# Sample mixer's tail: scores stored, the dense blocks' top-k moved into it, and their transposed input handed on through memory

## The chip, the cores and the metric

One core of one Trainium2 chip runs the whole program. The metric is the device time of one execution in microseconds (us).

## The reference, cut to what matters

Two layers, each a token mixer and then an expert channel mixer (PEER). 128 prompt tokens and 512 sample tokens go through both; the change concerns the sample tokens alone. For the channel mixer each token has 8 heads; a head has two queries of 128 numbers, each is scored against 128 keys, the best 16 of each half are combined and the best 16 pairs name 16 experts. So a token reads 128 rows of `u` and 128 rows of `v`.

```python
def peer(h, wq, sub_keys, u, v):
    ...
    def one_block(xt):                      # 128 tokens
        q = (xt @ wq).reshape(PEER_BLOCK, PEER_HEADS, 2, PEER_HALF)
        s = jnp.einsum('thpd,pnd->thpn', q, sub_keys).astype(jnp.float32)
        s1, i1 = lax.top_k(s[:, :, 0], PEER_TOPK)
        s2, i2 = lax.top_k(s[:, :, 1], PEER_TOPK)
        cand = (s1[..., :, None] + s2[..., None, :]).reshape(PEER_BLOCK, PEER_HEADS, PEER_TOPK * PEER_TOPK)
        sc, ci = lax.top_k(cand, PEER_TOPK)
        idx = jnp.take_along_axis(i1, ci // PEER_TOPK, axis=-1) * N_KEYS + jnp.take_along_axis(i2, ci % PEER_TOPK, axis=-1)
        g = jax.nn.softmax(sc, axis=-1)
        a = jax.nn.gelu(jnp.einsum('td,thkd->thk', xt, u[idx]).astype(jnp.float32))
        return jnp.einsum('thk,thkd->td', (g * a).astype(xt.dtype), v[idx])
...
    x = layer_norm(ALPHA * x + gate1 * mix, ln1_g, ln1_b)
    h = x * (1.0 + scale2) + shift2
    x = layer_norm(ALPHA * x + gate2 * peer(h, peer_wq, peer_sub_keys, peer_u, peer_v), ln2_g, ln2_b)
```

## The kernel before, in words

**Blocks.** The 512 sample tokens are four blocks of 128. Blocks 0 and 1 (`ROWS`, called r0 and r1 here) are done row by row: GpSimd (POOL) gathers one `u` or `v` row per token into a tile `gat` (128x1024, half a megabyte), and VectorE (DVE) takes one dot product (L917) or one multiply-add (L947) with it. A block has 128 `u` rows and 128 `v` rows, and six `gat` tiles (`GB`). Blocks 2 and 3 (`DENSE`, called d0 and d1) are done densely: TensorE (PE) multiplies their 256 tokens with all 128 x 128 experts, 128 experts ("a key") at a time. `uc` is such a slab of `u`, `hp` its product; a `v` slab is accumulated into `vacc`. In between DVE and PE build the sparse weights: DVE makes `A`, `eq` and `bw` for 16 tokens, PE multiplies them to `Gp` (L1070), DVE multiplies that into the activations `Q` (L1075). `spread(c)` does this for a quarter of the keys in 16 such groups, 64 groups a layer. The first group needs the top-k of d0 and d1 finished: their indices go through `ki`, `kf` and a PE transpose `kT`.

**A front** is the top-k of one block: for each of 8 heads two times `top16` (L797 to L802: MAX8, FIND_INDEX8, MATCH_REPLACE8, MAX8, FIND_INDEX8) over the scores `sc`, then the 50 candidate pairs, a third `top16`, and three operations on 800 numbers (`oh`, `oh`, `xf`) that fetch the index. Heads are done in groups: r0 in groups of 1, 1, 2, 2, 2 (`LEAD`), the others in two groups of 4. A group ends with its indices `idx`, which the gathers need.

**The tail** of the sample mixer computes the queries: for each head, `qp` from eight slabs of weights that ScalarE (ACT) and DVE or POOL split into a high part `wh` and a low part `wl`, copied by ACT to `q` and stored to `qTd` in DRAM. While it runs, DVE does the front of r0, whose scores PE takes straight from `q` ("near"), and the first `U0` = 56 rows of `u` for r0.

**The dense stage** follows: `dense` loads the `h2` rows of d0 and d1, transposes them on PE into `h2Td`, and starts with the `hp` of 32 keys. The fronts of d0, d1 and r1 lie in this stage. Each head of such a front loads `qT` from DRAM, PE multiplies it with the keys into `sc` in PSUM (L825), and DVE's `top16` reads that. The `sc` tiles share two PSUM buffers with `hp`, `Gp` and `kT`, and PE takes its instructions in order.

**Order.** The program is written as generators that `weave` interleaves by shares of a nominal length; a scheduler at build time then moves instructions within what their data allow. The result is one fixed order for each engine and queue. In layer 0 the prompt's mixer of layer 1 is woven into the dense stage; in layer 1 the dense stage stands alone and ends the program.

In the profile, layer 0 has its tail at 1428 us and its first `bw` at 1852 us, the seventeenth `bw` (the first of the second quarter) at 1961 us, and its last `vacc` at 2986 us. In layer 1 these are 4064, 4488, 4612 and 5405 us.

## Time and profile before

| | us |
|---|---|
| three timed runs | 5451.07, 5448.35, 5431.43 |
| their median | 5448.35 |
| the profiled execution, its own time | 5425.23 |
| its span, first to last instruction | 5423.5 |
| mean granted TensorE clock of the span | 0.887 of full speed |

The profile is of one execution, 23 us faster than the median of the three timed ones. The busy time of an engine is the time in which at least one of its instructions was running; what an engine waited for is inferred from semaphores. A wait counts only where that engine is the one that everything else waits for.

### The profile page before, as it was taken

To read this page: it belongs to the slowest core of one execution; us is meant where nothing else is said; L and a number is where in the kernel's file an instruction comes from. 1 tells how busy PE (TensorE), PEld (TensorE's weight loads), DVE (VectorE), ACT (ScalarE), POOL (GpSimd) and SP (SyncE) were. 2 spreads that over 40 slices of the span, in tenths; PEclk is the share of its full clock that TensorE was granted. 3 is DMA by queue.
4 is the path that set the end of the run, shared out by engine and by line. 5 is a ranking of instruction groups with operands and counts; after the bars stand their busy time and mean duration, and the time that the engine had idled before them with its cause. 6 is when DMAs were issued, how large, how long until landed. Compare 5 with 4: busy or idle time off the path is not lost.

```text
span 5423.5 us, 71661 instructions
## 1 busy us (share of the span) xinstructions
PE 4479.1 (83%) x26668; PEld 3365.0 (62%) x26668; DVE 3891.9 (72%) x8020; ACT 1038.4 (19%) x1876; POOL 2199.4 (41%) x1632
## 2 busy tenths in 40 slices
PE   7979878877766789799999477688977458998998
PEld 5658766755655657567674355588765347675643
DVE  4242578887699987948565999963258999979682
ACT  4231223412212101110000312255221010000000
POOL 0000026675255541544431576610115657255440
PEclk8989977888878889899999778789988779998999
DMA  5325669898489887899995788820447989699985
GB/s 185 118 70 179 235 225 327 305 338 297 171 318 348 317 317 258 310 357 334 382 344 206 244 309 297 290 91 29 131 146 271 329 305 362 225 399 325 409 327 197
DMA packets 472734, 1440.70 MB, mean 266 GB/s; under 512 B 55232, under 2 KB 123968, under 8 KB 472384
## 3 DMA queue, kind: packets, MB, share of 16 engines
q0 software_dynamic: 221184, 805.40, 40.5%
q1 hardware_dynamic: 251200, 630.71, 33.0%
q8 instruction: 209, 3.42, 0.2%
q14 instruction: 141, 1.16, 0.1%
HBM read 1391.29 MB, written 44.63 MB: 265 GB/s over the span
## 4 chain that ended last, share of the span: by engine, by line
PE 39%; DVE 26%; DMA 15%; issue 14%; POOL 4%; ACT 2%; SPq 0%; DVEq 0%; POOLq 0%; ACTq 0%
PE vacc L1096 7%; DVE gat L917 7%; PE gt L156 6%; PE proj L156 6%; DMA gat<-in_pv,idx 5%; PE hp L156 4%; DMA gat<-in_pu,idx 4%; POOL gat L900 4%; DVE acc L947 4%; PE po L156 3%; PE qp L156 2%; DMA v<-in_pv 2%; PE s L156 1%; PE gqk L156 1%; DVE A L1055 1%
## 5 line engine op out<-in xcount | busy, mean ns | idle before, releaser
L900 POOL DMA_INDIRECT gat<-in_pu,idx x768 | 982.3, 1279 | 884.9 <-DVE gat L917 378.7
L900 POOL DMA_INDIRECT gat<-in_pv,idx x768 | 989.4, 1288 | 765.1 <-DVE acc L947 472.9
L947 DVE SCALAR_TENSOR_TENSOR acc<-gat,dots,acc 128x1024 f32<-128x1024 f32 x762 | 1006.3, 1321 | 168.3 <-DMA gat<-in_pv,idx 156.1
L917 DVE SCALAR_TENSOR_TENSOR gat<-gat,h 128x1024 f32<-128x1024 f32 x768 | 948.4, 1247 | 110.8 <-DMA gat<-in_pu,idx 109.5
L156 PE MATMUL hp<-h2Td,uc 128*128 128x256 f32 x4096 | 942.5, 391 | 79.8 <-DVE wk L800 49.6
L1096 PE MATMUL vacc<-v,Q 128*128 128x512 f32 x2048 | 923.3, 604 | 17.2 <-DMA v<-in_pv 17.2
L156 PEld LDWEIGHTS hp<-h2Td,uc 128*128 128x128 f32 x4096 | 795.3, 196 | 200.2 <-DVE wk L800 52.3
L141 POOL TENSOR_TENSOR wl<-w,wh 128x1024 fp32r<-128x1024 f32 x92 | 227.5, 2473 | 1450.0 <-ACT wh L139 1279.5
L1096 PEld LDWEIGHTS vacc<-v,Q 128*128 128x128 f32 x2048 | 384.1, 193 | 459.4 <-issue 435.4
L139 ACT ACTIVATE wh<-w 128x1024 fp32r<-128x1024 f32 x184 | 194.4, 1058 | 631.9 <-PE proj L156 299.1
L1009 ACT ACTIVATE Q<-hp 128x512 f32<-128x512 f32 x128 | 76.4, 597 | 1069.6 <-PE hp L156 1069.3
L156 PE MATMUL proj<-wh,hTh 128*128 128x256 f32 x896 | 265.6, 296 | 5.6 <-DVE sgo L497 2.9
L156 PE MATMUL proj<-wl,hTh 128*128 128x256 f32 x896 | 264.7, 295 | 5.5 <-POOL wl L141 5.4
L156 PE MATMUL proj<-wh,hTl 128*128 128x256 f32 x896 | 262.8, 293 | 0.0
L1070 PEld LDWEIGHTS <-A 128*128 128x128 bf16 x6144 | 172.8, 97 | 125.7 <-DVE bw L1063 63.2
L156 PE MATMUL po<-V,pT 128*128 128x64 f32 x1600 | 237.9, 294 | 9.9 <-ACT pT L639 9.8
L156 PEld LDWEIGHTS po<-V,pT 128*128 128x128 f32 x1600 | 229.2, 217 | 24.9 <-ACT pT L639 16.7
L1070 PE MATMUL Gp<-bw,A 128*128 128x32 bf16 x6144 | 175.8, 177 | 73.3 <-DVE bw L1063 64.1
L141 DVE TENSOR_TENSOR wl<-w,wh 128x1024 fp32r<-128x1024 f32 x92 | 121.0, 1315 | 158.7 <-ACT wh L139 148.4
L629 DVE TENSOR_REDUCE nm<-s 128x1 f32<-128x768 f32 (+1 forms) x160 | 131.0, 820 | 139.9 <-PE s L156 138.5
L156 PEld LDWEIGHTS proj<-wh,hTh 128*128 128x128 f32 x896 | 176.9, 197 | 20.4 <-issue 16.2
L156 PEld LDWEIGHTS proj<-wl,hTh 128*128 128x128 f32 x896 | 176.9, 197 | 20.4 <-issue 13.8
(297 smaller groups left out, 7355.5 us busy)
## 6 DMA issues: line engine op xcount, KB each, us to landing
uc<-in_put SPq DMA_DIRECT2D x256, 512.0 KB, 7.0
v<-in_pv SPq DMA_DIRECT2D x256, 512.0 KB, 6.7
w<-in_win SPq DMA_DIRECT2D x208, 512.0 KB, 5.1
w<-in_adaw SPq DMA_DIRECT2D x96, 512.0 KB, 5.7
w<-in_wq SPq DMA_DIRECT2D x64, 512.0 KB, 5.8
w<-in_wgo SPq DMA_DIRECT2D x32, 512.0 KB, 5.5
w<-in_wao SPq DMA_DIRECT2D x32, 512.0 KB, 5.2
w<-in_wout SPq DMA_DIRECT2D x32, 512.0 KB, 5.5
```

What stands on the lines that cost most here:

```text
L139: nc.scalar.activation(wh, r, AF.Copy)
L141: (nc.vector, nc.gpsimd)[i].tensor_sub(wl, r, f32(wh))
L156: nc.tensor.matmul(out, lt, rt, start=(i == 0), stop=(i == n - 1))
L629: nc.vector.tensor_reduce(nm, s[:, 0:KEYS], axis=AX.X, op=OP.max, negate=True)
L900: i = nc.gpsimd.indirect_dma_start(out=t, out_offset=None, in_=src, in_offset=bass.IndirectOffsetOnAxis(ap=self.res[b][0][:, k:k + 1], axi ...
L917: nc.vector.scalar_tensor_tensor(u, u, 1.0, h2, op0=OP.mult, op1=OP.mult, accum_out=dots[:, k:k + 1])
L947: nc.vector.scalar_tensor_tensor(acc, v, w_, acc, op0=OP.mult, op1=OP.add)
L1009: nc.scalar.activation(q[:, i:i + 2, :].rearrange("p i t -> p (i t)"), t, AF.Gelu_apprx_tanh)
L1055: nc.vector.tensor_tensor(a.rearrange("p t (i w) -> p t i w", w=2), pairs[:, None].to_broadcast([128, TG, NK // 2, 2]), i1[:, sl, None, :] ...
L1070: nc.tensor.matmul(t[:, j * CI:(j + 1) * CI], a[:, j, :], bw[:, j, q, :], start=(q == 0), stop=(q == 2))
L1096: nc.tensor.matmul(accs[i][:, s * 512:(s + 1) * 512], w[:, j, i * 128:(i + 1) * 128], v[:, s * 512:(s + 1) * 512], start=(key == 0), stop= ...
```

## The change

It touches the sample tokens alone, in both layers. Lines in this section and in the order rows of the change are those of the changed file.

- In the tail, PE multiplies each head's `q` with the keys at once, for all four blocks (L812). ACT copies the scores from PSUM to a tile `sc` in SBUF, and stores those of r1, d0 and d1 to `scd` in DRAM, a DMA that ACT issues itself (L821). The `qTd` stores of the sample and the `qT` loads go.
- The fronts of d0, d1 and r1 load these scores back into `scs` (two buffers), also from ACT's queue (L852); their `top16` reads SBUF.
- d0 and d1 are done in four groups of two heads (`NEXT`). Three of the four groups of each are written into the tail, between the groups of r0; the fourth opens the dense stage.
- Of r0's `u` rows 24 in place of 56 are written into the tail (`U0`).
- The tail copies the transposed `h2` of d0 and d1 a second time from PSUM (`hc`, ACT), stores it, and `dense` loads it with one DMA of 1 MB. The `h2` rows of d0 and d1 are no longer stored, loaded or transposed again.

```diff
...
 LEAD = (1, 1, 2, 2, 2)
+NEXT = (2, 2, 2, 2)
-FF = (0.05, 0.1, 0.3, 0.46)
+FF = (0.01, 0.02, 0.3, 0.46)
 DENSE = (2, 3)
...
-U0 = 56
+U0 = 24
...
-    x_dram, x1_dram, h2_dram, tops = {}, {}, {}, {}
+    x_dram, x1_dram, h2_dram, h2t_dram, tops = {}, {}, {}, {}, {}
...
         x1d = dram.tile([T, D], F32, name=f"x1d{tr}{l}")
         h2d = dram.tile([T, D], F32, name=f"h2d{tr}{l}")
         x1_dram[tr, l], h2_dram[tr, l] = x1d, h2d
+        if tr:
+            h2t_dram[l] = dram.tile([128, ND, len(DENSE) * 128], F32, name=f"h2t{l}")
...
         if tr == 0 and l == 0:
             yield from ada(l, (GATE1, SCALE2, SHIFT2, GATE2), W)
-        qTd = dram.tile([2 * PH, 128, T], F32, name=f"qTd{tr}{l}")
-        tops[tr, l] = qTd
+        if tr:
+            scd = dram.tile([nb, 128, PH * 2 * NK], F32, name=f"scd{l}")
+            tops[tr, l] = scd
+        else:
+            qTd = dram.tile([2 * PH, 128, T], F32, name=f"qTd{tr}{l}")
+            tops[tr, l] = qTd
         with mkp("out") as op:
             r = op.tile([128, nb, D], F32, name="r")
             x = op.tile([128, nb, D], F32, name="x")
...
                     h2 = spare("h2")
                     nc.vector.tensor_mul(h2, rb, s2)
                     nc.vector.tensor_add(h2, h2, sh)
-                    nc.sync.dma_start(h2d[b * 128:(b + 1) * 128, :], h2)
+                    kept = tr == 1 and b in DENSE
+                    if not kept:
+                        nc.sync.dma_start(h2d[b * 128:(b + 1) * 128, :], h2)
                     for j0 in range(0, ND, jg):
                         t = ptile("h2t")
                         for j in range(jg):
...
                             put_split(dst, t3)
                         else:
                             evac(dst[0], t3)
+                        if kept:
+                            hc = spare("hc")
+                            nc.scalar.activation(hc[:, 0:jg * 128], t, AF.Copy)
+                            i = DENSE.index(b)
+                            nc.sync.dma_start(h2t_dram[l][:, j0:j0 + jg, i * 128:(i + 1) * 128],
+                                              hc[:, 0:jg * 128].rearrange("p (j t) -> p j t", j=jg))
                     yield 6
                 for b in range(nb):
                     rb, xb = r[:, b, :], x[:, b, :]
...
             for h in range(PH):
                 w = W(wq[l, h])
                 t = ptile("qp")
+                qs = []
                 for k in range(2):
                     projT(t[:, k * off:k * off + T], w, k, h2T)
-                    q = hp.tile([128, T], F32, tag="q", bufs=2 + 2 * tr, name="q")
+                    q = hp.tile([128, T], F32, tag="q", bufs=2 + tr, name="q")
                     if tr:
                         nc.scalar.activation(q, t[:, k * off:k * off + T], AF.Copy)
                     else:
                         evac(q, t[:, k * off:k * off + T])
-                    nc.sync.dma_start(qTd[2 * h + k], q)
-                    lp[l]["q", tr, 2 * h + k] = q
+                        nc.sync.dma_start(qTd[2 * h + k], q)
+                    qs.append(q)
+                if tr:
+                    yield 11
+                    for b0 in range(0, nb, 2):
+                        s = psm("sc", 1)
+                        for i in range(2):
+                            for k in range(2):
+                                nc.tensor.matmul(s[:, (2 * i + k) * NK:(2 * i + k + 1) * NK],
+                                                 qs[k][:, (b0 + i) * 128:(b0 + i + 1) * 128],
+                                                 lp[l]["sk"][:, k, :], start=True, stop=True)
+                        sc = hp.tile([128, 2, 2 * NK], F32, tag="sc", bufs=4, name="sc")
+                        nc.scalar.activation(sc.rearrange("p b n -> p (b n)"), s, AF.Copy)
+                        for i in range(2):
+                            if b0 + i == ROWS[0]:
+                                lp[l]["s", h] = sc[:, i, :]
+                            else:
+                                nc.scalar.dma_start(scd[b0 + i, :, h * 2 * NK:(h + 1) * 2 * NK], sc[:, i, :])
                 lp[l]["qp", tr] = h + 1
-                yield 11
+                yield 3 if tr else 11
             hs.close()
             ys_.close()
...
                 hh = h0 + h
                 assert lp[l]["qp", tr] > hh
                 if near:
-                    qs = [lp[l]["q", tr, 2 * hh + k][:, b * 128:(b + 1) * 128] for k in range(2)]
+                    s = lp[l]["s", hh]
+                elif tr:
+                    s = own.tile([128, 2 * NK], F32, tag="scs", bufs=2, name="scs")
+                    nc.scalar.dma_start(s, tops[tr, l][b, :, hh * 2 * NK:(hh + 1) * 2 * NK])
                 else:
                     qT = sm.tile([128, 2, 128], F32, tag="qT", bufs=CB, name="qT")
                     nc.sync.dma_start(qT, tops[tr, l][2 * hh:2 * hh + 2, :, b * 128:(b + 1) * 128]
                                       .rearrange("k p t -> p k t"))
-                    qs = [qT[:, k, :] for k in range(2)]
-                s = psm("sc", tr)
-                for k in range(2):
-                    nc.tensor.matmul(s[:, k * NK:(k + 1) * NK], qs[k], lp[l]["sk"][:, k, :], start=True, stop=True)
+                    s = psm("sc", tr)
+                    for k in range(2):
+                        nc.tensor.matmul(s[:, k * NK:(k + 1) * NK], qT[:, k, :], lp[l]["sk"][:, k, :],
+                                         start=True, stop=True)
                 for k in range(2):
                     top16(tv[:, h, k, :], ti[:, h, k, :], s[:, k * NK:(k + 1) * NK], NK)
                 yield 2
...
             CI, QB, HI, UB = CIS[self.l], QBS[self.l], HIS[self.l], UBS[self.l]
             per = CI // HI
             h2T = dp.tile([128, ND, T], F32, name="h2Td")
-            for i, b in enumerate(blocks):
-                x = dp.tile([128, D], F32, tag="uv", bufs=UB, name="x")
-                nc.sync.dma_start(x, h2_dram[self.tr, self.l][b * 128:(b + 1) * 128, :])
-                t = psb("h2td")
-                for j in range(ND):
-                    nc.tensor.transpose(t[:, j * 128:(j + 1) * 128], x[:, j * 128:(j + 1) * 128], ident)
-                evac(h2T[:, :, i * 128:(i + 1) * 128], t.rearrange("p (j t) -> p j t", j=ND))
-                yield 4
+            nc.sync.dma_start(h2T, h2t_dram[self.l])
+            yield 4
             Q = {}
             def acts(hf):
...
             parts["p_close", l].close()
             p = Peer(1, l, opener(st_, 0)("sgat"), GB)
             r0, r1 = ROWS
-            d0, d1 = DENSE
             f0, u0 = p.front(r0, LEAD, True), p.u_rows(r0)
+            fd = [p.front(d, NEXT) for d in DENSE]
             def lead():
-                for n in LEAD:
-                    yield from take(m, n)
+                for i, n in enumerate(LEAD):
+                    yield from take(m, 2 * n)
                     yield from take(f0, 3 * n + 1)
+                    if i >= 2:
+                        for f in fd:
+                            yield from take(f, 3 * NEXT[i - 2] + 1)
                 for _ in m:
                     pass
-            yield from weave([(lead(), 160.0, 0.0, 1.0)], [(take(u0, U0), 1.5 * U0, UP, 1.0)])
+            yield from weave([(lead(), 260.0, 0.0, 1.0)], [(take(u0, U0), 1.5 * U0, UP, 1.0)])
             for _ in f0:
                 pass
             ms.close()
...
             yield from weave([(p.dense(p.up, DENSE), 1010.0, DF[0], DF[1])],
                              [(u0, 192.0 - 1.5 * U0, r[0], r[1]), (p.v_rows(r0), 197.0, r[1], r[2]),
                               (p.u_rows(r1), 192.0, r[2], r[3]), (p.v_rows(r1), 197.0, r[3], r[4])],
-                             [(p.front(d0), 50.0, 0.0, f[0]), (p.front(d1), 50.0, f[0], f[1]),
-                              (p.front(r1), 50.0, f[2], f[3])])
+                             [(fd[0], 12.5, 0.0, f[0]), (fd[1], 12.5, f[0], f[1]), (p.front(r1), 50.0, f[2], f[3])])
         fs = parts["fin"] = ExitStack()
         fp = opener(fs, 0)("fin")
         ds.close()
```

What this does to PE's order at the start of layer 1's dense stage. Before, from the tail's last scores on (`qT` are the loaded queries of d0, then d1):

```order
L825 MATMUL sc<-sk,q 128x128 x2
L825 MATMUL sc<-sk,qT 128x128 x2
L995 MATMUL h2td<-ident,x 128x128 x16
L825 MATMUL sc<-sk,qT 128x128 x6
L156 MATMUL hp<-h2Td,uc 128x256 x43
L825 MATMUL sc<-sk,qT 128x128 x2
L156 MATMUL hp<-h2Td,uc 128x256 x5
L825 MATMUL sc<-sk,qT 128x128 x4
L156 MATMUL hp<-h2Td,uc 128x256 x16
```

Here the scores of d0 and d1 (`sc<-sk,qT`) and the transposes of their `h2` (`h2td`) stand between and ahead of the `hp`.

After, the same place up to the transposes of the finished indices:

```order
L157 MATMUL qp<-h2Th,wl 128x512
L812 MATMUL sc<-sk,q 128x128 x8
L157 MATMUL hp<-h2Td,uc 128x256 x256
L1067 MATMUL kT<-ident,kf 128x128 x2
L1068 MATMUL kT<-ident,g 128x128
```

Eight `hp` are one key, so 32 keys stand ahead of `kT`, as before; what has moved is the scores, which now stand in the tail, before the `hp`.

DVE in layer 1, the last rows ahead of the first `bw`. Before, a stretch from the last index of d1 on, in which every second row is one of r0's `v` rows:

```order
L866 CAST idx<-xf 128x64
L947 SCALAR_TENSOR_TENSOR acc<-gat,dots,acc 128x1024
L1033 TENSOR_SCALAR ki<-idx 128x128
L947 SCALAR_TENSOR_TENSOR acc<-gat,dots,acc 128x1024
L1037 CAST kf<-ki 128x128
L947 SCALAR_TENSOR_TENSOR acc<-gat,dots,acc 128x1024
```

Here nothing of r1 stands ahead of the first `bw`.

After, a stretch of the same place; `scs` now holds scores of r1, whose front stands between the rows that the first `bw` needs (`gt`, `gparts`):

```order
L1071 TENSOR_SCALAR gt<-kT 128x128
L982 SCALAR_TENSOR_TENSOR acc<-gat,dots,acc 128x1024
L829 MAX tv<-scs 128x8 x2
L896 TENSOR_TENSOR oh<-oh,cidx 128x800
L834 MAX_INDEX ti<-tv,wk 128x8
L1074 CAST gparts<-gt 128x256x2
L982 SCALAR_TENSOR_TENSOR acc<-gat,dots,acc 128x1024
L830 MAX_INDEX ti<-tv,scs 128x8
L832 MATCH_REPLACE wk<-tv,scs 128x128
```

Operations of r1's front have moved ahead of `gparts`, and with it ahead of the first `bw`.

ACT in layer 1 after the change, at the end of the tail and the start of the dense stage, with what each instruction waits for (`g` is the softmax of a group, `Q` the activation of two keys, which frees their PSUM buffer):

```order
L904 ACTIVATE g<-g 128x32 [waits DVE_49]
L852 DMA scs<-scd_29526 128x256 [waits DMAHW5_49,DVE_49]
L852 DMA scs<-scd_29526 128x256 [waits DMAHW6_49,DMAHW0_49,DVE_49]
L904 ACTIVATE g<-g 128x32 [waits DVE_49] x2
L852 DMA scs<-scd_29526 128x256 [waits DMAHW7_49,DVE_49]
L852 DMA scs<-scd_29526 128x256 [waits DMAHW0_49,DVE_49]
L1038 ACT_TABLE_LOAD [waits PE_49]
L1038 ACTIVATE Q<-hp 128x512 [waits Pool_49]
```

Before, ACT had no DMA to issue, and the first `Q` stood behind softmaxes alone; now the loads that wait until DVE has freed a buffer stand ahead of it too.

## Rows read from the trace of the kernel before

**Rows 1.** The page: span, and part 1, busy time of the engines.
```profile
span 5423.5 us, 71661 instructions
PE 4479.1 (83%) x26668; PEld 3365.0 (62%) x26668; DVE 3891.9 (72%) x8020; ACT 1038.4 (19%) x1876; POOL 2199.4 (41%) x1632
```

**Rows 2.** Windows: stretch, length, busy PE, PEld, DVE, ACT, POOL, clock, DMA share, GB/s.
```profile
1428.00:1852.00 424.00, 300.99 (x1296) 243.81 (x1297) 396.53 (x1278) 83.69 (x151) 236.62 (x175) 0.83 0.85 307
1852.00:1961.00 109.00, 95.80 (x1078) 78.78 (x1077) 105.36 (x137) 14.37 (x30) 52.19 (x41) 0.91 0.83 302
1961.00:2986.00 1025.00, 960.45 (x5766) 653.89 (x5767) 693.34 (x1361) 79.48 (x162) 382.05 (x304) 0.96 0.85 315
4064.00:4488.00 424.00, 246.08 (x1013) 200.19 (x1013) 395.14 (x1193) 49.39 (x70) 252.78 (x190) 0.78 0.84 300
4488.00:4612.00 124.00, 122.44 (x1197) 108.44 (x1198) 123.04 (x135) 8.37 (x14) 88.25 (x59) 0.97 0.98 365
4612.00:5405.00 793.00, 750.79 (x4469) 466.25 (x4467) 572.10 (x953) 29.78 (x44) 328.13 (x271) 0.97 0.85 320
5000.00:5200.00 200.00, 195.27 (x1077) 131.82 (x1076) 140.76 (x144) 9.70 (x16) 95.85 (x91) 0.98 0.98 383
```

**Rows 3.** PE's waits in 4064 to 4488 us: total us, times, longest.
```profile
PE sc L825 <- DVE wk L800: 43.8, 4, 17.7
PE sc L825 <- DMA qT<-qTd: 39.7, 6, 8.3
PE kT L1038 <- DVE kf L1037: 26.3, 2, 24.2
```

**Rows 4.** DVE's waits in 4064 to 4488 us: total us, times, longest.
```profile
DVE wl L141 <- ACT wh L139: 16.3, 1, 16.3
```

**Rows 5.** Groups of DVE instructions by form, whole span: count | busy us, mean ns.
```profile
L797 DVE MAX8 tv<-sc 128x8 f32<-128x128 f32 x160 | 45.8, 287 | 53.3 <-PE sc L825 53.2
L798 DVE FIND_INDEX8 ti<-tv,sc 128x8 uint32<-128x128 f32 x160 | 45.8, 286 | 0.0
L798 DVE FIND_INDEX8 si<-sv,cand 128x8 uint32<-128x50 f32 x80 | 15.7, 199 | 0.0
L861 DVE TENSOR_TENSOR oh<-oh,cidx 128x800 f32<-128x800 f32 x80 | 79.8, 998 | 0.2
L843 DVE TENSOR_TENSOR cidx<-iff 128x32 f32<-128x32 f32 x38 | 6.8, 180 | 0.0
```

**Rows 6.** Timeline of DVE, layer 1, around the first bw: start us, length us.
```profile
4472.16 1.28 DVE L947 SCALAR_TENSOR_TENSOR acc<-gat,dots,acc 128x1024 f32<-128x1024 f32 x1
4473.36 0.22 DVE L1037 CAST kf<-ki 128x128 f32<-128x128 int32 x1
...
4488.46 1.82 DVE L1063 TENSOR_TENSOR bw<-eq,gparts 128x1536 bf16<-128x1536 bf16 x2
```

**Rows 7.** Timeline, layer 1: r0's first index, the first u row after it, a value load.
```profile
4091.68 1.23 DVE L866 CAST idx<-xf 128x16 int32<-128x16 f32 x1
...
4101.92 1.23 DVE L917 SCALAR_TENSOR_TENSOR gat<-gat,h 128x1024 f32<-128x1024 f32 x1 [3.38 <-DMA gat<-in_pu,idx]
...
4103.07 0.09 DVE L802 MATCH_VALUE_LOAD ti<-tv,wk 128x8 f32 x1
```

**Rows 8.** DMA issues of 4064 to 4488 us: count, KB each, us to landing.
```profile
qTd<-q SPq DMA_DIRECT2D x16, 256.0 KB, 4.8
qT<-qTd SPq DMA_DIRECT2D x17, 128.0 KB, 4.2
```

**Rows 9.** ACT's copy of a transposed block, by its tile h2Th: ns.
```profile
L271 ACT ACTIVATE h2Th<-h2t x8: 1024/1024/1025, 1412.2 to 4062.2; 128x1024 fp32r<-128x1024 f32 x8
```

**Rows 10.** PE's waits in 1961 to 2986 us: total us, times, longest.
```profile
PE Gp L1070 <- DVE bw L1063: 23.1, 5, 11.1
...
PE sc L825 <- DVE wk L800: 4.1, 2, 2.7
```

**Rows 11.** PE's waits in 4612 to 5405 us, same columns.
```profile
PE Gp L1070 <- DVE bw L1063: 23.1, 8, 8.1
```

## The prediction, made before the changed kernel had run

> **What bounds it now.** I read the page first [rows 1], then the windows by stage [rows 2], then the waits of PE and DVE in the stage that changes. Over the span PE is the busiest engine, with 4479 of 5423 us. The windows show two regimes that this average mixes. From a tail's start to the first `bw` (424 us in either layer) DVE is busy 397 and 395 us, PE only 301 and 246 [rows 2]. From the seventeenth `bw` on it is the other way round: PE 960 of 1025 and 751 of 793, DVE 693 and 572 [rows 2]. So DVE's instructions, done in order, set when the first quarter of the sparse weights begins; PE's work sets how long it takes from there to the end. Between the two, to the seventeenth `bw`, DVE is still full (105 of 109, 123 of 124), and in layer 1 PE with it [rows 2].
>
> In 4064 to 4488 us PE waits 43.8 us for DVE's replace (`wk`), because `sc` holds PSUM until `top16` has read it, and 39.7 us for `qT` [rows 3]. The change takes both away. But PE has 32 keys of `hp` ahead of `kT` and `Gp` before and after it, as the order shows, and then stands waiting for DVE's `kf` (24.2 us at once [rows 3]). What PE saves ahead of `kT` lengthens that wait. The time of the first groups follows from what DVE has to do ahead of them.
>
> **What DVE has to do up to the seventeenth bw.** By the order, all 128 `u` rows of r0 and the fronts of r0, d0 and d1 are done by the first `bw` before and after; 24 rows in place of 56 in the tail only moves 32 of them within this stretch. Three things change.
>
> The front of r1 comes forward. Before none of it, after most of it stands ahead of the first `bw`, and all of it ahead of the seventeenth, in both layers. Its price: DVE starts an instruction about 0.08 us before the one ahead has ended (4472.16 and 1.28 against 4473.36 [rows 6]), so I take 0.08 off each mean; a find or a replace is preceded by a value load of 0.09 us [rows 7] and so keeps its full mean. A head has 4 MAX8 at 0.287 less 0.08, 6 finds and replaces at 0.28, on the 50 candidates 5 operations of 0.84 together (0.12 for a MAX8, 0.20 for the rest), and three of 800 numbers at 0.998 less 0.08 [rows 5]: 0.83 + 1.68 + 0.84 + 2.75 = 6.1 us. A group adds about 23 small operations at 0.18 less 0.08 [rows 5], 2.3 us. Eight heads and two groups are 49 + 5 = 54 us.
>
> d0 and d1 have four groups each in place of two: 4 × 2.3 = 9 us.
>
> Against it, r0's `v` rows go back: by the order 59 in place of 74 stand ahead of the seventeenth `bw` in layer 0, 66 in place of 107 in layer 1. A row costs 1.28 less 0.08 = 1.2 us [rows 6], which makes 18 and 49 us.
>
> DVE's other rows there come to some 4 us fewer. In all 54 + 9 − 18 − 4 = **+41 us in layer 0** and 54 + 9 − 49 − 4 = +10, of which I keep **+9 in layer 1**, where the order's rows, each at the mean of its kind, sum a little lower.
>
> **New waits.** `idx` to the first use of a gathered row took 4101.92 − 4091.68 = 10.2 us [rows 7]. The changed order puts three `u` rows that open a new index group only 5.0, 5.9 and 5.9 us of DVE work behind their `idx`; the lack is 4 to 5 us each, 14 in sum, less what DVE's starts drift: **13 us a layer**. Bounds: nothing, if gathers land faster here, to 14.
>
> `hc` is one more ACT copy of the kind of `h2Th`, 1.02 us [rows 9], between the transposes that the tail's first `qp` need: **1 us a layer**, bounds 0 to 2, for two blocks.
>
> Each score load must follow its store: 4.8 us to land what was stored and 4.2 to land a block of 128 KB [rows 8]. With two buffers, the second next head's load is issued when DVE has freed one, and a head is 6 us of DVE work with `u` or `v` rows between; the order leaves 9 to 16 us. I take nothing. If the cover fails everywhere, it is 9 us for each of the 8 groups of d0 and d1, 72 us a layer. One row comes near this: `qT`, also stored and loaded, cost PE 39.7 us in 6 waits [rows 3], but that was a wait of PE, while DVE was 395 of 424 us busy all the same.
>
> What leaves: sixteen `qTd` stores of 256 KB and some 24 loads of 128 KB make way for 24 stores and 24 loads of 128 KB, and `h2` for one 1 MB load. The DMA share of the stage is 0.84 [rows 2], so I count no gain for it. PE's 48 more score matmuls lie in the tail, where PE is idle a third of the time [rows 2].
>
> In layer 0 the order also has PE one key of `hp` and 18 matmuls of the prompt short at the seventeenth `bw`; that work falls after it. A key is 8 `hp`, and at some 0.17 us each (960 us for 5766 matmuls [rows 2]) with the prompt's 18 wider ones it is **7 us**.
>
> **What comes back behind it.** After the seventeenth `bw` PE idles 1025 − 960 = 65 us in layer 0 and 793 − 751 = 42 in layer 1 [rows 2]. With r1's front gone from there DVE is earlier for each `bw`, and PE's instructions are the same. In layer 0 `Gp` waits 23.1 us for `bw` and scores for `wk` another 4.1 [rows 10]; I give back these, **28 us**. In layer 1 the same wait is 23.1 [rows 11], but the DMA share is 0.98 in 5000 to 5200 [rows 2], and 30 more gathers of half a megabyte now fall behind the first `bw`; that would make PE late for `v`. I give back **15**. Bounds: nothing, to the whole 107 us.
>
> **Sum.** Layer 0: 41 + 1 + 13 + 7 − 28 = +34. Layer 1: 9 + 1 + 13 − 15 = +8. Together +42 us, on the profiled execution 5425 + 42 = 5467. That execution lies 23 us under the median of the three timed runs, so against the median I say 5448 + 42 = **5490 us**. A difference under 0.5%, 27 us, is about what a measurement of this kernel cannot tell from none.
>
> A rule speaks on where the price of the scores could lie. The row: `scs` loads stand in ACT's order with a wait on DVE, ahead of `g` and `Q`. The Trainium skill, page "DMA: Bandwidth & Descriptors", section "Anatomy of one DMA — SWDGE (gpsimd) path", says that DMA engines do not wait on semaphores: a wait is held on the sequencer that issues the transfer. By it everything behind such a load on ACT stands still until DVE has freed the buffer; no row of before shows it, since ACT issued no DMA there. The sum would then grow towards rival C.
>
> **Rivals.**
>
> A, the forecast: the first groups come later by DVE's extra work, and only a part is given back. Its own range: with half the gather waits and all the measured waits given back, about +15; with 5 us given back in each layer, +75. That is 5463 to 5523. Chance 0.45.
>
> B, faster. PE closes its idle time after the seventeenth `bw`, since DVE has nothing of r1's front there to do. Then 41 + 9 + 2 + 7 − 107 = −48, 5400 us. It decides once more than 59 of those 107 us come back and no new wait adds to it. For it: DVE's share falls there and its `bw` are PE's longest wait [rows 10, 11]. Against it: these waits are 46 us together, and the rest of the idle time is many short gaps, which an earlier DVE does not touch. Chance 0.15.
>
> C, much slower. ACT becomes the bound of the tail. Its queue now holds stores, loads that wait for DVE, and behind them the softmax, the copies of `q` and the `wh` that the next head's `qp` need. Already before, DVE waited 16.3 us at once for `wh` [rows 4]. If half of the 72 us above are paid in each layer, it is +42 + 72 = +114, 5562 us. For it: ACT and DVE then wait for each other in turn, at each head. Against it: ACT is busy only 84 and 49 of 424 us [rows 2]. Chance 0.20.
>
> D, nothing that can be measured. No gather wait shows, and half of the idle time comes back: 41 + 9 + 2 + 7 − 53 = +6, 5454 us. The change then does move the fronts, and DVE's total is nearly the same. Chance 0.20.
>
> **How the numbers follow.** A is likeliest, so 5490. Four fifths of A lie above 27 us, 0.36, the rest is no change; with C slower is 0.56, with D the same is 0.29, and B leaves 0.15. For 8 in 10 the range takes in A and D, half of C up to its price (5560) and the part of B near its turning point, from 5410.
>
> **What the profile after would show.** From the tail's start to the first `bw` 424 becomes about 465 us in layer 0 and 445 in layer 1, with DVE at least 93% busy. DVE waits for `gat` after three `idx` rows; PE's waits of `sc` for `wk` and of `sc` for `qT` are gone, and `kT` waits longer for `kf`. Behind the seventeenth `bw` PE's waits for `bw` shrink by about half. I am wrong if the first `bw` comes earlier or at its old time, if DVE has idle time that is put down to `scs` or to ACT (then C), or if PE's idle time behind the seventeenth `bw` goes under 50 us for both layers (then B or D).

## The result, and the profile after

The changed kernel takes 5482.54 us (median of five, 5475.07 to 5487.06) beside 5448.35 us before (median of five, 5431.43 to 5451.07). The ratio is 1.0068, 95% interval [1.0053, 1.0084]: slower by about 37 us. The forecast was 5490 us.

The page of the changed kernel, span and busy times, beside [rows 1]:

```profile
span 5485.3 us, 71803 instructions
PE 4456.2 (81%) x26636; PEld 3352.0 (61%) x26636; DVE 3903.2 (71%) x8202; ACT 1070.5 (20%) x1925; POOL 2207.9 (40%) x1632
```

The two profiled spans are 62 us apart, more than the timed runs: the changed kernel's profiled execution is the slowest of its five, and that of the kernel before (5425.23 us) lies under all its five. Part of the difference stands outside the changed stages. The first `h2Th` of layer 0, up to which nothing has changed, comes at 1412.2 us before and 1421.9 after; over all the kernels profiled here it lies between 1398 and 1422, so this is what one execution differs from another. Another 9 us lie between layer 0's last `vacc` and layer 1's first `h2Th`. So I count from the tail on, stage by stage. The windows of the changed kernel answer to [rows 2]: tail to first `bw`, to the seventeenth, to the last `vacc`, for each layer.

```profile
1442.00:1900.00 458.00, 271.21 (x1248) 223.57 (x1249) 423.48 (x1542) 100.76 (x172) 214.03 (x166) 0.79 0.77 273
1900.00:2019.00 119.00, 104.14 (x1111) 86.93 (x1111) 115.76 (x203) 17.09 (x36) 48.34 (x35) 0.90 0.72 248
2019.00:3019.00 1000.00, 958.24 (x5770) 650.06 (x5767) 660.22 (x1105) 76.17 (x159) 393.03 (x319) 0.97 0.90 331
4109.00:4544.00 435.00, 235.66 (x1030) 195.84 (x1030) 399.48 (x1448) 62.60 (x93) 206.99 (x162) 0.76 0.74 261
4544.00:4676.00 132.00, 126.77 (x1202) 111.66 (x1203) 125.54 (x192) 11.20 (x17) 93.05 (x47) 0.97 0.83 290
4676.00:5467.00 791.00, 748.50 (x4433) 461.15 (x4431) 574.29 (x733) 24.25 (x38) 379.78 (x312) 0.97 0.92 346
```

Read the DVE column (third of the busy times). Up to the seventeenth `bw` DVE is 423.5 + 115.8 = 539.2 us busy in layer 0 against 396.5 + 105.4 = 501.9 before, so 37 us more, and 525.0 against 518.2 in layer 1, 7 more. The rows gave 41 and 9. The stretch grew with it, from 424 + 109 to 458 + 119 us and from 424 + 124 to 435 + 132. Behind it layer 0 is 25 us shorter (1025 to 1000), layer 1 only 3 (793.4 to 790.4 before the windows are rounded).

What PE waits for in layer 1, tail to first `bw`, answers to [rows 3]:

```profile
PE hp L157 <- ACT Q L1038: 84.7, 4, 78.0
PE hp L157 <- DMA uc<-in_put: 62.9, 4, 29.2
PE kT L1067 <- DVE kf L1066: 18.8, 2, 10.2
```

The waits of `sc` for `wk` and `qT` (83.5 us) are gone, and others (147.6 us for `Q` and `uc`) stand in their place. The largest, 78 us at once, is for the first `Q`: it frees the PSUM of two keys, and ACT reaches it 280 us behind the tail's first `qp`, where it was 182 and 191 us before. ACT's timeline shows what stands ahead of it, and for comparison the next score load, which is issued alone:

```profile
4382.49 0.23 ACT L904 ACTIVATE g<-g 128x32 f32<-128x32 f32 x1 [26.14 <-DVE g L903]
4383.10 4.68 ACTq L852 DMA_DIRECT2D scs<-scd  x2
4387.86 1.28 ACT L1038 ACT_TABLE_LOAD   x1 [5.14 <-DVE g L909]
4389.16 0.60 ACT L1038 ACTIVATE Q<-hp 128x512 f32<-128x512 f32 x1
...
4396.71 0.33 ACTq L852 DMA_DIRECT2D scs<-scd  x1
```

A softmax waits for DVE, then two score loads do, then comes `Q`. ACT's waits for DVE's `g`, the inputs of the softmaxes, from the tail's first `qp` to the first `bw` of layer 1, before and after:

```profile
ACT g L869 <- DVE g L868: 57.9, 9, 21.5
...
ACT g L904 <- DVE g L903: 210.8, 14, 43.0
```

So ACT does hold `Q` behind instructions that wait for DVE, as rival C feared for the copies of `q` and the `wh`, and the softmaxes are a large part of them. The question of the experiments is whether that time shows.

DVE's own waits in the same stretch, after (against [rows 4]), which show no wait for `scs`:

```profile
DVE wl L142 <- ACT wh L140: 15.8, 1, 15.8
DVE gat L952 <- DMA gat<-in_pu,idx: 14.4, 13, 3.8
DVE tv L829 <- ACT sc L816: 5.1, 2, 2.7
```

### The profile page after: what moved, and what is told of

Same layout as the page of the kernel before. It is cut to its first block, busy times and chain, and to the rows that moved or that the text cites. A ratio compares the mean times of both kernels' runs of the same rounds, so it can differ in the third digit from the quotient of the medians.

```text
span 5485.3 us, 71803 instructions
## 1 busy us (share of the span) xinstructions
PE 4456.2 (81%) x26636; PEld 3352.0 (61%) x26636; DVE 3903.2 (71%) x8202; ACT 1070.5 (20%) x1925; POOL 2207.9 (40%) x1632
## 4 chain that ended last, share of the span: by engine, by line
PE 36%; DVE 30%; DMA 13%; issue 13%; POOL 5%; ACT 3%; SPq 0%; another core or an unknown queue 0%; POOLq 0%; DVEq 0%; ACTq 0%
DVE gat L952 7%; PE proj L157 7%; DMA gat<-in_pv,idx 6%; PE gt L157 6%; PE vacc L1125 6%; POOL gat L935 4%; PE hp L157 4%; DVE acc L982 3%; DMA gat<-in_pu,idx 3%; PE po L157 3%; DVE A L1084 2%; DVE Q L1104 2%; PE s L157 1%; DVE bw L1092 1%; PE gqk L157 1%
## 5 line engine op out<-in xcount | busy, mean ns | idle before, releaser
L935 POOL DMA_INDIRECT gat<-in_pv,idx x768 | 1001.7, 1304 | 868.6 <-DVE acc L982 542.4
```

Source lines behind the costliest of these rows:

```text
L935: i = nc.gpsimd.indirect_dma_start(out=t, out_offset=None, in_=src, in_offset=bass.IndirectOffsetOnAxis(ap=self.res[b][0][:, k:k + 1], axi ...
```

## The experiments

The letters here are the experiments' own, not those of the prediction's rivals. Two theories. **D**: DVE's work in its fixed order sets the first `bw`, above all r1's front, which came forward. **A**: ACT's queue holds `Q`, so PE and with it `kT` are late. A third, **H**, is on the price of `hc`; **E**, which comes in with the hold, says that behind the first `bw` DVE or the gathers become the bound and the rows end late. Each experiment is an edit of the changed kernel, if not said otherwise, and each ratio is to the kernel before on the same chip. The medians of before were 5428 to 5444 us there, so the kernels are compared by ratios; the changed kernel's is 1.0068, and 0.1% is 5.4 us.

What the trace shows of each, in us from the tail's first `qp` (taken from the timelines of PE, ACT and DVE), layer 0 / layer 1:

| kernel | ratio | first Q | first bw | 17th bw | last vacc |
|---|---|---|---|---|---|
| before | 1 | 182 / 191 | 423 / 425 | 533 / 549 | 1558 / 1342 |
| changed | 1.0068 | 280 / 280 | 457 / 435 | 577 / 568 | 1577 / 1358 |
| sp_loads | 1.0064 | 284 / 276 | 461 / 435 | 577 / 562 | 1579 / 1345 |
| r1_old | 0.9966 | 276 / 278 | 429 / 399 | 540 / 522 | 1549 / 1330 |
| next44 | 0.9983 | 271 / 267 | 440 / 420 | 553 / 546 | 1548 / 1335 |
| no_h2t | 1.0024 | 287 / 284 | 455 / 435 | 572 / 563 | 1564 / 1350 |
| hc_own | 1.0039 | 279 / 280 | 456 / 435 | 575 / 563 | 1580 / 1359 |
| after_gp | 1.0022 | 283 / 270 | 452 / 421 | 567 / 551 | 1569 / 1341 |
| combo | 0.9905 | 274 / 266 | 424 / 389 | 542 / 513 | 1552 / 1323 |
| combo72 | 0.9959 | 244 / 237 | 372 / 346 | 506 / 474 | 1523 / 1271 |
| combo104 | 0.9998 | 276 / 269 | 406 / 382 | 527 / 510 | 1549 / 1303 |
| combo104gp | 1.0017 | 271 / 271 | 405 / 388 | 522 / 514 | 1545 / 1306 |
| before72bw | 0.9893 | 183 / 191 | 352 / 336 | 481 / 460 | 1488 / 1263 |
| before104bw | 0.9844 | 182 / 192 | 370 / 362 | 478 / 487 | 1508 / 1300 |

Two kernels with the same order of rows on DVE (changed and sp_loads) differ by 13 us in layer 1's last column: a stage of one profiled execution is no sharper than that.

**r1_old: r1 alone the old way.**

```diff
+                    if tr:
+                        nc.sync.dma_start(q1d[2 * h + k], q[:, 128:256])
...
-                            else:
+                            elif b0 + i != ROWS[1]:
                                 nc.scalar.dma_start(scd[b0 + i, ...
...
-                elif tr:
+                elif tr and b != ROWS[1]:
                     s = own.tile([128, 2 * NK], F32, tag="scs", ...
```

> Only r1 goes back to the old way: its queries are stored, loaded, and multiplied with the keys late, on PE. DVE's order then has 45 us (layer 0) and 40 us (layer 1) less work ahead of the first bw than the changed kernel (sums of rows, each at its mean duration before). Theory D, DVE's work in order sets the first bw: first bw 35 to 45 us earlier in both layers; layer 0 gives back about half of that as it did with the change, layer 1 nearly none of it, so 50 to 65 us faster than the changed kernel, 5418 to 5433 us, under the kernel before. Rival A, ACT's queue sets it (PE waited 78 us at once for an ACT copy that stands behind score loads and softmaxes): these stand there for d0 and d1 as in the changed kernel, first bw at most 10 us earlier, 5465 to 5482 us.

Measured 0.9966 [0.9954, 0.9978], 1.0% or 55 us below the changed kernel. The first `bw` comes 29 and 36 us earlier, the end 28 in each layer. D's line had 35 to 45 us, and nearly nothing given back in layer 1, where 18 of the 46 us that were won up to the seventeenth `bw` went again. The time is D's result; A's 5465 us and more would have been a ratio above 1.003. The first `Q` did not move (276, 278).

**sp_loads: the score loads on SP.**

```diff
-                    nc.scalar.dma_start(s, tops[tr, l][b, :, ...
+                    nc.sync.dma_start(s, tops[tr, l][b, :, ...
```

> The score loads of d0, d1 and r1 are issued by SP in place of ACT; DVE's order stays as it is, row for row. Theory D: first bw at the same time within 8 us, 5474 to 5490 us, though PE's wait of hp for Q gets shorter. Rival A: PE's wait of hp for Q (84.7 us in layer 1) falls by half or more and the first bw comes 15 us or more earlier, under 5460 us. A third way: SP's loads of uc now stand behind score loads that wait for DVE, PE's wait of hp for uc (62.9 us) grows by more than what Q's falls, over 5490 us.

Measured 1.0064 [1.0044, 1.0084], the same as the changed kernel. PE's waits in layer 1, tail to first `bw`:

```profile
PE hp L157 <- DMA uc<-in_put: 149.1, 4, 105.6
PE kT L1067 <- DVE kf L1066: 19.0, 2, 10.3
...
PE hp L157 <- ACT Q L1038: 3.2, 2, 2.5
```

ACT's wait for the softmaxes' inputs in the same stretch:

```profile
ACT g L904 <- DVE g L903: 201.9, 14, 44.1
```

The wait for `Q` is gone from this view, and one for `uc` has its place, since SP's `uc` loads now stand behind the score loads; the first `Q` is where it was. ACT waits for the softmaxes' inputs nearly as long as in the changed kernel (201.9 us beside 210.8), so the loads were not what kept it. `kT` waits 19 us for `kf` as in the changed kernel. So of each line a part holds: the wait for `Q` fell by more than half, as A had it, the wait for `uc` grew by 86 us, as the third had it, PE was not freed, and the time is D's. A label of a wait moved, and nothing else.

**next44: d0 and d1 in two groups of four heads.**

```diff
-NEXT = (2, 2, 2, 2)
+NEXT = (4, 4)
...
-                    if i >= 2:
+                    if i == 3:
                         for f in fd:
-                            yield from take(f, 3 * NEXT[i - 2] + 1)
+                            yield from take(f, 3 * NEXT[0] + 1)
```

> d0 and d1 in two groups of four heads in place of four groups of two; the first groups lie in the tail with its fourth group of r0. DVE's rows ahead of the first bw sum to 21 us less in layer 0 and 16 less in layer 1. Theory D: first bw 12 to 20 us earlier in both, end 18 to 30 us earlier, 5453 to 5465 us. Rival A: groups of four finish later, so the softmaxes on ACT, and Q behind them, wait longer for DVE; first bw not earlier, 5478 to 5500 us.

Measured 0.9983 [0.9967, 0.9998], 0.85% or 46 us below the changed kernel, more than D's 18 to 30. The seventeenth `bw` is 24 and 22 us earlier and the end 28 and 23: of the lateness that this takes away, nothing had been given back.

**no_h2t and hc_own: what the h2 part costs.** The first undoes the h2 part; the second gives `hc` a buffer.

```diff
-                            hc = spare("hc")
+                            hc = op.tile([128, D], F32, tag="hc", bufs=1, name="hc")
```

> The h2 part alone is undone: h2 rows of d0 and d1 are stored, loaded and transposed again on PE as before, the second copies (hc) go. Theory H: the four copies of hc delayed the tail's start by 4 us a layer, PE's sixteen transposes lie in its idle time: first bw 3 to 5 us earlier in each layer, 5474 to 5480 us. Rival: the early load of the whole input is worth something (hp starts sooner), then hp starts later and the time is 5482 to 5495 us.

> The second copy hc gets a buffer of its own; in the changed kernel it takes a turn in h2's ring of two, and the last block's h2 has to wait for the third block's. Theory H: that is the whole of what the h2 part costs at the tail's start; from the first h2Th to the first qp 16 to 17 us as before the change in place of 20.3, 5 to 10 us faster than the changed kernel. Rival: the copies themselves or their stores cost it, then 20 us stay and the time is within 3 us of the changed kernel's.

Measured 1.0024 [1.0010, 1.0038] and 1.0039 [1.0025, 1.0054], some 24 and 16 us below the changed kernel. From the first `h2Th` to the first `qp` it is 16.2 us before, 20.4 in the changed kernel, 16.2 without the h2 part, and 17.1 and 17.3 with the buffer. The timelines of ACT, then DVE, of the changed kernel show the wait:

```profile
4100.86 1.02 ACT L272 ACTIVATE h2Th<-h2t 128x1024 fp32r<-128x1024 f32 x1 [6.92 <-PE h2t L771]
4103.18 1.02 ACT L781 ACTIVATE hc<-h2t 128x1024 f32<-128x1024 f32 x1 [1.29 <-DVE h2Tl L273]
4107.66 1.02 ACT L272 ACTIVATE h2Th<-h2t 128x1024 fp32r<-128x1024 f32 x1 [3.46 <-PE h2t L771]
...
4101.92 1.22 DVE L273 TENSOR_TENSOR h2Tl<-h2t,h2Th 128x1024 fp32r<-128x1024 f32 x1 [3.18 <-ACT h2Th L272]
4103.06 1.22 DVE L763 TENSOR_TENSOR h<-r,lv 128x1024 f32<-128x1024 f32 x1
```

and ACT's of hc_own, without it:

```profile
4096.53 1.02 ACT L272 ACTIVATE h2Th<-h2t 128x1024 fp32r<-128x1024 f32 x1 [8.04 <-PE h2t L771]
4098.23 1.02 ACT L272 ACTIVATE h2Th<-h2t 128x1024 fp32r<-128x1024 f32 x1 [0.68 <-PE h2t L771]
```

`hc` takes a turn in `h2`'s ring of two. The last block's `h<-r,lv` then finds no free buffer until the third block is transposed, and the last two `h2Th` lie 6.8 us apart in place of 1.7. H holds: 3.1 to 3.3 us a layer are the ring, 0.9 to 1.0 the copy. The 6 us a run that the ring explains, and the 8 of ring and copy, are less than the 16 and 24 that the ratios give, which lie above both expectations; with 0.2% between two of these ratios, some 11 us, I leave the rest open.

**combo: r1_old, next44 and hc_own together.**

> r1 the old way, d0 and d1 in two groups of four, hc in a buffer of its own. DVE's rows ahead of the first bw sum to 375 and 349 us, against 429 and 404 in the changed kernel and 400 and 399 before. Theory D: first bw 45 to 55 us earlier than in the changed kernel in both layers, 75 to 90 us faster than it, a ratio to the kernel before of 0.990 to 0.993. Rival A: PE, held by ACT's queue, reaches kT later than DVE has kf ready, and stops the gain at what r1 alone gave: ratio 0.995 to 0.997.

Measured 0.9905 [0.9888, 0.9923], 1.6% or 89 us below the changed kernel, as D had it; with 51 us it is also faster than the kernel before. The first `bw` came 33 and 45 us earlier, in layer 0 less than D's 45 to 55: there DVE is 375 of 424 us busy, 88% in place of 92%, a first sign that something else holds it too.

**The hold: 72 of r0's u rows ahead of the first bw.** If D is right, `u` rows should be held back as well. In both kernels DVE's remaining `u` rows of r0 are ordered behind the first `bw`, and the `v` rows follow.

```diff
-U0 = 24
+U0 = 72
...
-                nc.vector.scalar_tensor_tensor(u, u, 1.0, h2, ...
+                with tc.issue_after(self.gate) if self.tr == 1 and b == ROWS[0] and k >= 72 else nullcontext():
+                    nc.vector.scalar_tensor_tensor(u, u, 1.0, h2, ...
...
+                    if c == 0 and t0 == 0:
+                        self.gate = bwi.ins
```

(In the kernel before `U0` was 56; the share of the dense stage at which the other rows start is 0.13, and 0.14 there, in place of 0.02.)

> As the combination, and 72 of r0's u rows ahead of the first bw, the other 56 and all v rows held behind it in DVE's order. DVE's rows ahead of the first bw sum to 277 and 266 us. Theory D: first bw 60 to 100 us earlier than in the combination (PE's 32 keys may stop it), and as DVE is 600 to 715 us busy of 800 to 1008 behind the seventeenth bw, 100 us more of rows fit there: the end comes 40 us or more earlier per layer, ratio under 0.975. Rival E: behind the first bw DVE or the gathers become the bound, r1's v rows end late, and most of it is lost: ratio 0.98 to 1.00.

> The kernel before, nothing of the change in it, with the same hold: 72 u rows ahead of the first bw, the rest behind it. DVE's rows ahead of the first bw sum to 284 and 267 us in place of 400 and 399. Theory D: the first bw comes 60 to 110 us earlier in each layer and the ratio is under 0.98; if the change's scores still wait on PSUM and qT, this kernel stays 10 to 40 us behind the combination with the hold. Rival E: ratio 0.98 to 1.00. Rival F, PE sets the first bw through qT and wk waits (83 us in layer 1): first bw less than 40 us earlier.

Measured 0.9959 [0.9943, 0.9974] and 0.9893 [0.9876, 0.9910]. The dense stage's end did come earlier, 29 and 52 us against the combination, 70 and 79 against before; the first `bw` came 53 and 43 us earlier than in the combination, not 60 to 100. It is E that keeps the time: the last window of combo72, from the last `vacc` to the end, has PE at nothing and DVE at its `v` rows.

```profile
5334.00:5419.00 85.00, 0.10 (x1) 0.00 (x0) 62.36 (x94) 3.61 (x3) 29.75 (x27) 0.52 0.68 248
```

In layer 0 as well r1's last `v` row ends behind the last `vacc` (23 us in combo72, 39 in before72bw; 74 us ahead of it in the combination, 101 before), and layer 1's first `h2Th` follows the last `vacc` by 1095 and 1096 us, in place of 1053 and 1060.

What neither theory had: combo72 is behind before72bw. DVE's waits in layer 1 ahead of the first `bw`, combo72:

```profile
DVE kf L1071 <- PE kT L1072: 45.0, 1, 45.0
```

and before72bw:

```profile
DVE tv L797 <- PE sc L825: 18.7, 9, 4.7
...
DVE kf L1038 <- PE kT L1039: 16.3, 1, 16.3
```

Here DVE waits for PE. In the changed kernel it was the other way round.

**The hold at 104.**

> The combination with 104 of r0's u rows ahead of the first bw, 24 and all v rows behind it. With 72 the dense stage of layer 1 ended 46 us earlier (by its start to its last vacc 1323 to 1271 us), but r1's last v row ended 67 us later and 50 us behind it, so the rows ended the program. Theory D with E as its limit: about 23 v and u rows less are moved than at 72 (32 u rows come back, 20 and 33 v rows go ahead of the seventeenth bw again), dense and rows end within 30 us of each other, ratio to the kernel before 0.980 to 0.988. Rival: no better than the combination, 0.989 to 0.992, since the 45 us in which DVE waited for kT with 72 stay with PE, which ACT's queue holds.

> The kernel before with the same hold at 104. Theory D with E: as the rows ended last with 72 (46 us behind the dense stage in layer 1), fewer held rows end the program earlier: ratio 0.984 to 0.989. If PE's waits for the stored queries bound it, 0.990 to 0.995. Beside the combination at 104 it shows what the changed kernel's parts are worth once DVE's rows don't hide PE: theory D wants the two within 0.4% of each other.

Measured 0.9998 [0.9986, 1.0010], which both lines missed, and 0.9844 [0.9827, 0.9862], as expected and the fastest of all, 85 us below the kernel before. D wanted the two within 0.4% and is refuted as the whole story: ahead of the first `bw` DVE is 319 and 307 us busy in the one and 326 and 311 in the other, yet in combo104 the first `bw` comes 36 and 20 us later. The first `Q` lies at 276 and 269 against 182 and 192, the sixteenth, behind which `kT` stands on PE, at 396 and 376 against 362 and 355. Beside the combination, combo104 is 20 us better in layer 1's dense stage, and loses that and more between layer 0's last `vacc` and layer 1's first `h2Th` (1084.9 us against 1053.5) and at the end, where its last `v` row is 18 us behind the last `vacc`. Why layer 1's mixer takes 31 us longer I have not settled; here r1's last `v` row of layer 0 ends 22 us ahead of the last `vacc`.

**after_gp and combo104gp: ACT's queue freed.** Loads from GpSimd into four buffers, one softmax a front.

```diff
-                    s = own.tile([128, 2 * NK], F32, tag="scs", bufs=2, name="scs")
-                    nc.scalar.dma_start(s, tops[tr, l][b, :, ...
+                    s = own.tile([128, 2 * NK], F32, tag="scs", bufs=4, name="scs")
+                    nc.gpsimd.dma_start(s, tops[tr, l][b, :, ...
...
+            if tr:
+                if h0 + n < PH:
+                    h0 += n
+                    res[b, 0] = h0 * TOPK
+                    yield 1
+                    continue
+                g, n = g_, PH - h0
```

> The changed kernel, with ACT's queue freed: the score loads of d0, d1 and r1 issued by GpSimd into four buffers, and one softmax for a whole front in place of one for each group, so that the first Q stands behind r0's softmax alone. DVE's rows ahead of the first bw sum to 12 us less in each layer (fewer small operations of the softmaxes). The first Q, 280 us behind the tail's first qp in both layers of the changed kernel, should come at 190 to 230. Theory D, DVE sets the first bw and PE only waits for it: 15 to 30 us faster than the changed kernel, no more than its own 12 us a layer give. Rival A, PE held by ACT shares in it: 35 to 60 us faster. Third: GpSimd's gathers wait behind score loads, DVE waits for gat, not faster than the changed kernel.

> The combination with the hold at 104, with ACT's queue freed in the same way. There DVE waited 38 us for kT in layer 1, and the sixteenth Q, behind which kT stands on PE, came 396 and 376 us behind the first qp, against 362 and 355 in the kernel before with the same hold. Rival A, which with DVE's rows held is now the theory: first Q at 190 to 230 in place of 276 and 269, sixteenth Q 15 to 40 us earlier, ratio to the kernel before 0.975 to 0.99. Theory D alone: DVE's rows are the same within 3 us, so nothing changes, 0.997 to 1.002.

Measured 1.0022 [1.0012, 1.0033], 25 us below the changed kernel and in D's range, and 1.0017 [1.0007, 1.0026], nothing gained on combo104. But the premise failed in both: the first `Q` stayed at 270 to 283 us. ACT's timeline of combo104gp:

```profile
4340.83 0.31 ACT L916 ACTIVATE g<-g 128x128 f32<-128x128 f32 x1 [150.05 <-DVE g L907]
4341.16 1.28 ACT L1051 ACT_TABLE_LOAD   x1
4342.46 1.08 ACT L1051 ACTIVATE Q<-hp 128x512 f32<-128x512 f32 x2
```

The loads and the small softmaxes have left, and r0's one softmax, which waits 150 us for DVE, holds `Q` as they did. In layer 1 PE's waits for `uc`, 86.8 us in combo104, are down to 10.5 us in combo104gp and the first `bw` is no earlier, so it was not `uc` that kept it. But these two runs don't tell whether an early `Q` would help; a kernel with `Q` ahead of every softmax was not tried.

## Why the prediction was right, and where not

**DVE's rows** were the step that carried it: +41 and +9 us forecast, +37 and +7 measured as DVE's busy time, and r1_old and next44 took the lateness away by taking rows away. The first `bw` was forecast at 465 and 445 us, and came at 457 and 435. DVE was 92% busy there, a shade under the 93% that I had asked for.

**The sum, +42, came out for two errors that cancel.** Counted from a layer's first `h2Th` to its last `vacc`, which leaves out the drift of the unchanged stages, layer 0 went from 1574.3 to 1596.9 us, +22.6 where I had +34, and layer 1 from 1358.5 to 1378.4, +19.9 where I had +8. That the total is right to a few us is luck. The terms:

- Gather waits, 13 us a layer, were too large for the `u` rows that I had in mind: DVE's waits for `gat` grew from 6.0 to 11.0 us and from 7.9 to 14.4, 5 and 6.5 us. In layer 1 a wait that I had not foreseen comes on top, for gathered `v` rows between the first and the seventeenth `bw`, where DVE had no wait before:

```profile
DVE acc L982 <- DMA gat<-in_pv,idx: 6.1, 2, 5.4
```

The forecast's 10.2 us came from one row; why half of the lack did not show is open (the DMA share of the two stretches fell to 0.77 and 0.74, from 0.85 and 0.84).

- `hc`, 1 us, was too small: 4.1 us. I priced the copy and overlooked the buffer that it takes from `h2`.
- The 7 us of PE work left over in layer 0 can't be seen: PE is 958 us busy behind the seventeenth `bw`, 960 before.
- The return in layer 0, 28 us, was 25. In layer 1 it was 3, not 15. PE's waits in 4676 to 5467 us, against [rows 11], show where it went:

```profile
PE Gp L1099 <- DVE bw L1092: 13.8, 8, 4.7
PE hp L157 <- DMA uc<-in_put: 8.6, 1, 8.6
PE Gp L1099 <- DVE Q L1104: 8.0, 2, 6.3
```

The wait for `bw` is 9 us shorter, as forecast, and a wait for `uc` of 8.6 us is new, in a stretch where the DMA share rose from 0.85 to 0.92. That gathers caused it is argued from that share, not shown.

With these sizes the terms close: 37 + 5 + 4 − 25 = 21 us in layer 0, beside 22.6, and 7 + 6.5 + 6.1 + 4 − 3 = 21 in layer 1, beside 19.9. The lower end of A's range was added up wrong: half the gather waits (13 us in all) and all the measured waits given back (50 us) leave 59 + 13 − 50 = +22, not +15.

**Two signs that I named were wrong.** `kT` was to wait longer for `kf`; it waited 18.8 us, not 26.3, since PE itself came late. And PE's idle time behind the seventeenth `bw` is 42 us in both layers, under the 50 that were to refute me, though the kernel is slower: in layer 1 it had been 42 before, so that bound could tell nothing.

**The rivals of the prediction.** B fell: of 107 us of idle time 22 came back, not 59. D, nothing that can be measured, fell with it: the gather waits came, and a fifth of the idle time returned, not half. C was right that ACT's queue would hold something, and wrong in what, through what, and at what price. The `q` and `wh` that it named cost PE's `qp` 0.7 and 0.8 us of waiting in layer 1's tail; `Q` was held, and PE waited 84.7 us for it. The loads that it named did not decide it: without them on ACT (sp_loads, after_gp, combo104gp) the first `Q` stayed where it was, behind softmaxes that wait for DVE. The Trainium skill, page "DMA: Bandwidth & Descriptors", section "Anatomy of one DMA — SWDGE (gpsimd) path", says that a semaphore wait is held on the sequencer that issues a transfer. ACT's rows above agree: the two score loads ahead of `Q` take up 4.68 us of its queue, a load alone 0.33. The wait for `Q` did not set the changed kernel's time in layer 1: DVE was later still, and PE stood another 18.8 us at `kT`, waiting for DVE's `kf`. With DVE's rows out of the way (combo72, combo104), DVE's wait for `kT` grew to 45 and 38 us in layer 1, where the kernel before with the same holds has 16 and 15. That ACT's hold of `Q` is what makes PE late there fits these rows, but no run freed `Q`, so it is not shown. DVE's rows were the changed kernel's bound, as theory D of the experiments had it, and they hid a second one close behind.

## What to carry to other kernels

Sum what the engine that is behind has to do in its order ahead of the point that others wait for; moving a wait of an engine that is early changes its label and not the time. When an engine's queue takes on instructions that wait for a late engine, look at what stands behind them, even if today something else hides it: it can be the next bound. And the row order itself was worth more than the change: holding 24 of 128 `u` rows and all `v` rows behind the first `bw` made the kernel before 1.6% faster, 5351 us.

## What the runs showed of the hardware

Nothing was unexpected in single instructions. A top-k that reads scores from SBUF costs about what it cost from PSUM: in the changed kernel MAX8 on 128x128 takes 275 ns from `scs`, 287 from PSUM before, and FIND_INDEX8 282 and 286 [rows 5]. The rows, by form:

```profile
L830 DVE FIND_INDEX8 ti<-tv,scs 128x8 uint32<-128x128 f32 x96 | 26.0, 282 | 0.0
L829 DVE MAX8 tv<-scs 128x8 f32<-128x128 f32 x96 | 22.0, 275 | 0.0
```
